# Another order for the eight chunks of the MLP down products: pairs 2 and 3 are multiplied last

## The chip, the cores and the metric

The kernel runs on one core of a Trainium2 chip. The metric is the device time of one execution in microseconds, and the median of several executions stands for a kernel. The core has a matrix engine (TensorE, PE in the profile; its weight loads are PEld), three engines for elementwise work (VectorE or DVE, ScalarE or ACT, GpSimd or POOL) and SyncE (SP), whose queue issues most of the transfers between the chip's memory (HBM) and the core's own memory (SBUF). PE writes its sums to a small memory of eight banks (PSUM). Each engine works through its own list of instructions in order. An instruction that waits holds up all that stand behind it on its engine.

## The reference, cut to what matters

One decoder layer over 2048 tokens of width 1024: a token mixer (an mLSTM beside an attention with latent keys), then an MLP, both between RMS norms. The change concerns the last line but one, the product with `w_down` (4096 x 1024).

```python
x = x + rmsnorm(mix, norm_post_mix[l])
m = rmsnorm(x, norm_pre_mlp[l])
y = jnp.square(jax.nn.relu(m @ w_up[l])) @ w_down[l]
x = x + rmsnorm(y, norm_post_mlp[l])
```

## The kernel before

All products are made in pieces of fp32r numbers: a matrix is split into a high part and a low part, and a product is three matmuls (high by high, high by low, low by high). The products of the MLP follow a scheme of Strassen and Winograd: the 2 x 2 blocks of a product take seven block products and some additions, before and behind.

The hidden width of 4096 is cut into 16 **pairs** `p` of two 128-wide blocks. The up phase (`up`) computes for each pair and each half `g` of the tokens the seven left factors that the down product needs, and stores them in HBM as `hd[p, g]`. For most pairs they are stored **whole**, as fp32 numbers. For the pairs in `TWOS = (2, 6, 10)` they are stored **in two parts**, already split into high and low, which is twice the bytes.

The down phase takes the pairs in eight **chunks** `c` of two (`e` = 0 and 1). A chunk has eight **units** `u`, and a unit makes two tiles of 128 tokens (rows `r` = 0 and 1, each as two halves of 512 columns, named y0_0 to y15_1 by tile and half). Three pieces of code matter:

- `hidden(c, u, e)` brings the seven factors of one pair to SBUF. A pair stored whole is one load (`hr`, 448 KB), then two casts on ACT for the high part (`hh0`, `hh1`, products 0 to 3 and 4 to 6) and two subtractions on DVE for the low part (`hl0`, `hl1`; L2613). A pair stored in two parts is four loads straight into the same tiles (L2597: `hh0` and `hl0` of 256 KB, `hh1` and `hl1` of 192 KB) and no work on ACT or DVE. Each of these tiles has two buffers, so a load or a cast waits until PE has used the tile of two units before.
- `down(c, u, ws)` issues the seven products 0 to 6 of a unit, six matmuls each (three for each pair), into three banks: X (products 0, 4, 5 and 6), Y (1 and 3) and Z (2). A sum in a bank is read by `into`, an addition on DVE into the result (`y<-d_..`, L2681), or by `aside`, a copy on ACT and an addition on POOL (L2696). Product 4 goes on in bank X behind product 0, product 5 behind 4, and 6 behind 5, so each of them waits until the one before has been read. In the last chunk's last unit all of this goes to DVE.
- `finish` runs in the last chunk only, once for each of the 16 tiles: two squares with sums on ACT, a power on POOL (L2745), then for 13 of the tiles two multiplications on DVE (`both`, L2754) and two accumulating stores on the POOL queue (L2757). The last three tiles (14, 11 and 15) get instead a gain (L2735, on POOL for tile 14), two additions on DVE (L2748) and plain stores on the SP queue (L2751).

The right factors, the weights of the next chunk, are made by `first_factors` on ACT (L2371) and DVE (L2341, L2374) while a chunk runs.

What comes when is set by a planner (`Plan`): each operation has an estimated duration, what it follows, the buffers it takes and a key, and the planner goes through a simulated time and picks for each engine the ready operation with the lowest key. Its choice is the order on each engine. The order of PE's products in the down phase is written out by hand (`line`): unit by unit 0, 1, then product 5 of the unit before, 2, 3, product 6 of the unit before, 4. Only the last unit differs: 0, 1, product 5 of the unit before, 4, 2, product 6 of the unit before, 5, 3, 6.

Of the kernel before, what the change touches and what calls it, by code (L numbers as in the profile page):

```python
# [47 lines left out]
EXL = 1.0  # L48
DWIDE = 128
PM_ = 2  # L50
FRESH = (5, 6, 7, 8, 12)
SPREAD = 60.0
LATE = 2000
# [206 lines left out]
def trunk(ctx: ExitStack, tc: tile.TileContext, x, xT, pos, wu, wout, wup, wdn, cols, rows, consts, edge, out, dbg=None):  # L260
# [11 lines left out]
    def sb(stack, name, bufs, side="left"):  # L272
        return stack.enter_context(tc.tile_pool(name=name, bufs=bufs, side=side, reuse_waits="tile"))

    def pp(stack, name, bufs, side="left"):
        return stack.enter_context(tc.tile_pool(name=name, bufs=bufs, side=side, space=PSUM, reuse_waits="tile"))
# [251 lines left out]
    def wsplit(b, u):  # L528
        if u == 0:
            return wboth(b)  # L530
        fresh = b == NB - 1 and u in FRESH
        if b > STB[u] and not fresh:
# [993 lines left out]
    def switch2():  # L1526

        s_x.close()
        pm.append(pp(pc, "pm", PM_))
        V[0] = sb(pc, "a3", 1).tile([P, NT, 4, 129], F32R, tag="V0", name="V0")  # L1530
# [20 lines left out]
    for name, bufs, when in (  # L1551
        ("q", 1, o_s1), ("m", PM_, o_s2), ("S", SB_, o_s3), ("o0", PO_, o_s3), ("o1", 1, o_s3), ("t", TB_, o_s3), ("th", 1, o_s3), ("tl", 1, o_s3), ("ph", HB_, o_s3), ("p", 1, o_s3), ("pl", LB_, o_s3), ("ot", 1, o_s3), ("ou", 1, o_s3),
        ("mp", 4, o_s1), ("mx", 2, o_s1), ("mr", 2, o_s1), ("rsm", 2, o_s3),
# [111 lines left out]
    def maxima(h, qb, keys):  # L1665
# [4 lines left out]
        def ring(i):  # L1670
            return "q" if (h, qb) in EARLY or i % (1 + PM_) == PM_ else "m"

# [901 lines left out]
    def hidden(c, u, e):  # L2574

        g, i = divmod(u, 4)
        p = 2 * c + e
        t = {}
        key = DN + 9.7 * (8 * c + u) + 2 * e
        first = c == 0 and u < 2  # L2580
# [64 lines left out]
    def down(c, u, ws):  # L2645
        g, i = divmod(u, 4)
        s = 8 * c + u
        key = DN + 9.7 * (8 * c + u)
        hs = [hidden(c, u, e) for e in range(2)]
        t = {}  # L2650
        nm = f"d{c}_{u}"
# [129 lines left out]
    for c in range(NCH):  # L2781
        ws = []
        for e in range(2):
            p = 2 * c + e
            ring = [f"w{WORDER[(14 * c + 7 * e + j) % (WB + W2B)]}" for j in range(7)]
            ws.append(first_factors(f"d{p}", DN + 77.6 * c + 3 * e, lambda e_, p=p: wdn[(2 * p + e_) * P : (2 * p + e_ + 1) * P, :], "down", ring, [o_w[KD - 1, 1]]))
        XP["rings"] = [f"w{WORDER[(14 * NCH + k) % (WB + W2B)]}" for k in range(WB + W2B - 14)]
        for u in range(8):
            down(c, u, ws)
# [77 lines left out]
def build(arrays, dbg=None):  # L2867
    import concourse.bacc as bacc

    nc = bacc.Bacc("TRN2", target_bir_lowering=False, num_devices=1)  # L2870
    args = [
        nc.dram_tensor(f"in_{n}_dram", v.shape, mybir.dt.from_np(v.dtype), kind="ExternalInput").ap() for n, v in arrays.items()
    ]
    out = nc.dram_tensor("out_0_dram", (SEQ, DM), F32, kind="ExternalOutput").ap()
    with tile.TileContext(nc) as tc:
        trunk(tc, *args, out, dbg=dbg)
    return nc
# [9 lines left out]
```

## Time and profile before

| | us |
|---|---|
| median of 3 runs (2381.45 to 2382.77) | 2382.29 |
| the profiled execution, its own time | 2380.29 |
| its span, first to last instruction | 2378.5 |
| granted TensorE clock, mean | 0.997 |
| ACT busy in the span | 1353.1 (57%) |
| POOL busy in the span | 813.1 (34%) |
| first matmul of the down phase, start | 1745.85 |

The profile is of one execution. A page gives the busy time of each engine over the whole span; the trace behind it can be asked for a stretch of time, for one engine's instructions in order, or for who waited for whom. Of rows that stand for one instruction the first number is its start, counted from the start of the span, and the second its duration in us. Names have lost their running numbers there: `d_6X` is bank X of unit 6 of whichever chunk runs, `d_7X` of unit 7.

### The profile page before, as it was taken

Reading aid. Unit: us, or ns where it says so; the run is one execution under the profiler, and the core shown is the slowest. Engines: PE = TensorE matmul, PEld = TensorE weight load, DVE = VectorE, ACT = ScalarE, POOL = GpSimd, SP = SyncE. Lnnn points to the kernel's source line nnn. Section 1 sums busy time; section 2 is a strip of 40 time slices with the busy share of each in tenths; the row PEclk is TensorE's granted clock in tenths of the full one; section 3 lists DMA queues with packets and bytes.
Section 4 is the critical chain, followed back from the end, with each engine's and each line's share of the span. In section 5 each row is a group of like instructions: output and inputs, shape, how many; then the busy total and the mean of one; then the engine's idle time right before and its main releaser. Section 6 shows DMA issues by size and latency. Waiting matters only on the chain.

```text
span 2378.5 us, 33991 instructions
## 1 busy us (share of the span) xinstructions
PE 2339.0 (98%) x10989; PEld 1894.3 (80%) x10989; DVE 1717.6 (72%) x3057; ACT 1353.1 (57%) x2581; POOL 813.1 (34%) x697
## 2 busy tenths in 40 slices
PE   9999999999999999999999999999999999999997
PEld 7777778777777777788788888888888888888885
DVE  6767665868888988548667778676675677776778
ACT  5636463447788878344666557656565343443454
POOL 1725343538888888222000000000000223222346
PEclk9999999999999999999999999999999999999999
DMA  7787979783522322667677797665664445345348
GB/s 282 237 315 253 330 261 335 222 205 83 132 65 65 82 49 51 197 218 264 214 233 230 220 289 239 197 178 165 196 202 142 143 142 177 125 148 169 129 138 171
DMA packets 341159, 445.34 MB, mean 187 GB/s; under 512 B 35730, under 2 KB 228174, under 8 KB 340974
## 3 DMA queue, kind: packets, MB, share of 16 engines
q1 hardware_dynamic: 337236, 436.35, 58.8%
q0 software_dynamic: 3744, 6.82, 2.0%
q8 instruction: 86, 1.41, 0.2%
q14 instruction: 93, 0.76, 0.1%
HBM read 291.79 MB, written 153.07 MB: 187 GB/s over the span
## 4 chain that ended last, share of the span: by engine, by line
PE 55%; DVE 1%; DMA 0%; issue 0%; ACT 0%; POOL 0%; DVEq 0%; SPq 0%; POOLq 0%; ACTq 0%
PE op L268 1%; PE op L270 1%; PE op L269 1%; PE d_4X L2658 1%; PE d_1X L2659 1%; PE d_2X L2658 1%; PE d_4X L2659 1%; PE d_3X L2659 1%; PE d_1X L2658 1%; PE d_3X L2658 1%; PE d_2X L2659 1%; PE d_1X L2660 1%; PE d_2X L2660 1%; PE d_3X L2660 1%; PE d_4X L2660 1%; PE d_6X L2658 1%
## 5 line engine op out<-in xcount | busy, mean ns | idle before, releaser
L2696 POOL TENSOR_TENSOR y<-vd_0X,y 128x512 f32<-128x512 f32 x7 | 10.6, 1518 | 726.7 <-ACT vd_0X L2693 726.7
L1813 POOL TENSOR_TENSOR t<-t,ph 128x512 f32<-128x512 f32 (+3 forms) x184 | 209.6, 1139 | 16.8 <-ACT ph L1776 6.7
L1776 ACT ACTIVATE ph<-S 128x512 fp32r<-128x512 f32 (+1 forms) x288 | 165.2, 573 | 80.5 <-PE S L270 29.4
L2608 ACT CAST hh<-hr 128x512 fp32r<-128x512 f32 (+1 forms) x208 | 116.4, 567 | 156.4 <-PE d_5X L2659 15.1
L1784 DVE TENSOR_TENSOR pl<-S,ph 128x512 fp32r<-128x512 f32 (+1 forms) x229 | 153.0, 671 | 35.0 <-ACT S L1780 28.8
L1695 DVE TENSOR_REDUCE mp<-m 128x1 f32<-128x512 f32 (+3 forms) x208 | 136.0, 665 | 26.9 <-PE m L1688 24.3
L2613 DVE TENSOR_TENSOR hl<-hr,hh 128x512 fp32r<-128x512 f32 (+1 forms) x208 | 133.2, 647 | 30.3 <-ACT hh L2608 23.7
L268 PE MATMUL mm<-xh,wh 128*128 128x512 f32 x352 | 143.4, 407 | 4.8 <-DVE gate L1257 3.0
L270 PE MATMUL mm<-xh,wl 128*128 128x512 f32 x352 | 138.0, 392 | 0.7 <-DVE wl L552 0.5
L269 PE MATMUL mm<-xl,wh 128*128 128x512 f32 x352 | 138.0, 392 | 0.0
L1780 ACT ACTIVATE S<-S 128x512 f32<-128x512 f32 (+1 forms) x229 | 133.9, 585 | 0.0
L268 PE MATMUL S<-QK 97*128 97x512 f32 (+2 forms) x320 | 119.2, 373 | 0.3 <-DVE pl L1784 0.2
L1798 PE MATMUL o<-ph,V 128*128 128x512 f32 (+2 forms) x320 | 117.4, 368 | 1.1 <-DVE ot L1872 0.8
L269 PE MATMUL S<-QK 97*128 97x512 f32 (+2 forms) x320 | 117.0, 366 | 0.0
L270 PE MATMUL S<-QK 97*128 97x512 f32 (+2 forms) x320 | 116.5, 364 | 0.0
L1688 PE MATMUL m<-QK 96*128 96x512 f32 (+3 forms) x320 | 112.5, 386 | 2.9 <-DVE mp L1695 1.9
L1801 PE MATMUL o<-pl,V 128*65 128x512 f32 (+2 forms) x320 | 112.5, 361 | 1.1 <-POOL pl L1784 1.1
L268 PE MATMUL op<-wo,hh 128*128 128x512 f32 x256 | 101.0, 394 | 0.1
L270 PE MATMUL op<-wo,hl 128*128 128x512 f32 x256 | 99.8, 390 | 0.0
L269 PE MATMUL op<-wo,hh 128*128 128x512 f32 x256 | 99.8, 390 | 0.0
L2447 ACT ACTIVATE t<-t 128x512 f32<-128x512 f32 x96 | 60.7, 632 | 65.0 <-DVE t L2442 64.5
L268 PEld LDWEIGHTS mm<-xh,wh 128*128 128x128 f32 x352 | 66.1, 188 | 21.3 <-DVE gate L1257 4.7
(6463 smaller groups left out, 7477.3 us busy)
## 6 DMA issues: line engine op xcount, KB each, us to landing
hr<-hd SPq DMA_DIRECT2D x100, 448.0 KB
wr<-in_wu_dram SPq DMA_DIRECT2D x68, 512.0 KB
hd<-t SPq DMA_DIRECT2D x128, 256.0 KB
hd<-ts SPq DMA_DIRECT2D x96, 256.0 KB
wl<-wparts SPq DMA_DIRECT2D x37, 512.0 KB
QK<-qkd SPq DMA_DIRECT2D x32, 512.0 KB
xt<-in_x_dram SPq DMA_DIRECT2D x28, 512.0 KB
xf<-xd SPq DMA_DIRECT2D x40, 256.0 KB
```

The costliest lines, as they stand in the source:

```text
L268: pe.matmul(o, ah, bh, start=start, stop=False)
L269: pe.matmul(o, ah, bl, start=False, stop=False)
L270: pe.matmul(o, al, bh, start=False, stop=stop)
L1695: vec.tensor_reduce(mp["t"][:, j, kb : kb + 1], ps[:, :n], axis=AX.X, op=ALU.max)
L1776: act.activation(t["h"][:, :w], t["S"][:, :w], AF.Exp)
L1780: act.activation(t["p"][:, :w], t["S"][:, :w], AF.Exp)
L1784: (pool if by_pool else vec).tensor_tensor(t["l"][:, :w], t["p"][:, :w], f32(t["h"][:, :w]), ALU.subtract)
L1798: pe.matmul(o0, v[:, 0:128], t["h"][:, c : c + m], start=start, stop=stop)
L1813: pool.tensor_tensor(to, to, f32(t["h"][:, c : c + m]), ALU.add)
L2608: act.copy(t["h", m][:, :w], t["r", m][:, :w])
L2613: vec.tensor_tensor(t["l", m][:, :w], t["r", m][:, :w], f32(t["h", m][:, :w]), ALU.subtract)
L2658: pe.matmul(ps, a, w[:, 0], start=start, stop=False, skip_group_check=True)
```

## The change

The kernel gets a table of eight numbers. Position `c` of the down phase multiplies the pairs 2 * CHUNKS[c] and 2 * CHUNKS[c] + 1, where it multiplied 2c and 2c + 1. The pairs 2 and 3 go from the second place to the eighth, and the six chunks between move up by one. The sums are the same, in another order.

```diff
+CHUNKS = (0, 2, 3, 4, 5, 6, 7, 1)
 ...
     def hidden(c, u, e):
         g, i = divmod(u, 4)
-        p = 2 * c + e
+        p = 2 * CHUNKS[c] + e
 ...
     for c in range(NCH):
         ws = []
         for e in range(2):
-            p = 2 * c + e
+            p = 2 * CHUNKS[c] + e
```

The pairs stored in two parts are 2, 6 and 10, each the first of its chunk. The chunks that hold one were at the places 1, 3 and 5 (counted from 0) and are now at 2, 4 and 7. The order of PE's matmuls is the same row by row, with other factors. The other engines have the same instructions, at other places. Three places are shown; a row gives the line, the operation, and the result and operands with the program's names.

DVE in the last unit of the down phase, before. `y11_0<-d7_7X` is the reading of product 0 of unit 7, `y14_1<-d7_6X` that of product 5 of unit 6.

```order
L2681 TENSOR_TENSOR y10_1_18980<-d7_6X_23611,y10_1_18980 128x512
L2681 TENSOR_TENSOR y10_1_18980<-d7_6Y_23625,y10_1_18980 128x512
L2754 SCALAR_TENSOR_TENSOR y8_0_18760<-y8_0_18760,fsm8_23559,gpm_18466 128x512
L2754 SCALAR_TENSOR_TENSOR y8_1_18824<-y8_1_18824,fsm8_23559,gpm_18466 128x512
L2681 TENSOR_TENSOR y14_1_18920<-d7_6X_23611,y14_1_18920 128x512
L2754 SCALAR_TENSOR_TENSOR y12_0_18885<-y12_0_18885,fsm12_23608,gpm_18466 128x512
L2754 SCALAR_TENSOR_TENSOR y12_1_18768<-y12_1_18768,fsm12_23608,gpm_18466 128x512
L2681 TENSOR_TENSOR y11_0_18994<-d7_7X_23701,y11_0_18994 128x512
```

The same place after the change, where every line number is one higher:

```order
L2755 SCALAR_TENSOR_TENSOR y8_1_18824<-y8_1_18824,fsm8_23512,gpm_18466 128x512
L2682 TENSOR_TENSOR y13_0_18961<-d7_5X_23536,y13_0_18961 128x512
L2614 TENSOR_TENSOR hl1_7_7_1_23722<-hr_7_7_1_23549,hh1_7_7_1_23712 128x384
L2682 TENSOR_TENSOR y10_1_18976<-d7_6X_23630,y10_1_18976 128x512
L2682 TENSOR_TENSOR y10_1_18976<-d7_6Y_23643,y10_1_18976 128x512
L2755 SCALAR_TENSOR_TENSOR y12_0_18885<-y12_0_18885,fsm12_23588,gpm_18466 128x512
L2755 SCALAR_TENSOR_TENSOR y12_1_18768<-y12_1_18768,fsm12_23588,gpm_18466 128x512
L2682 TENSOR_TENSOR y11_0_18990<-d7_7X_23724,y11_0_18990 128x512
L2682 TENSOR_TENSOR y14_1_18920<-d7_6X_23630,y14_1_18920 128x512
```

The reading of product 0 of unit 7 now stands ahead of that of product 5 of unit 6, and the two multiplications for tile 8 stand further ahead. The last addition of all (`y15_0<-d7_7X`) had one multiplication of `both` behind it and now has two, both for tile 10.

DVE at the end of the second chunk, before (this chunk holds a pair in two parts; the rows begin behind the reading of unit 6's bank Y):

```order
L2374 TENSOR_TENSOR d46_19644<-d4s4_19281,d46_19644 128x512
L2341 TENSOR_TENSOR d5s2_19660<-d5r1_19357,d5s1_19393 128x512
L2374 TENSOR_TENSOR d50_19657<-d5r0_19356,d50_19657 128x512
L2613 TENSOR_TENSOR hl0_2_0_1_19683<-hr_2_0_1_19639,hh0_2_0_1_19676 128x512
L2681 TENSOR_TENSOR y14_1_18920<-d1_6X_19564,y14_1_18920 128x512
```

The same place after (this chunk holds two pairs stored whole):

```order
L2375 TENSOR_TENSOR d66_19660<-d6s4_19312,d66_19660 128x512
L2342 TENSOR_TENSOR d7s2_19679<-d7r1_19407,d7s1_19445 128x512
L2682 TENSOR_TENSOR y14_1_18920<-d1_6X_19568,y14_1_18920 128x512
L2614 TENSOR_TENSOR hl0_2_0_1_19699<-hr_2_0_1_19646,hh0_2_0_1_19687 128x512
L2682 TENSOR_TENSOR y11_0_18990<-d1_7Z_19689,y11_0_18990 128x512
```

The reading of bank X has two instructions ahead of it here instead of four. The four stand ahead of it at the end of every chunk with a pair in two parts that another chunk follows: three times before, twice after.

SP at the end of the last chunk, before, ahead of the six plain stores:

```order
L2601 DMA hr_7_5_1_23438<-hd15_1_217 128x896
L2601 DMA hr_7_6_0_23521<-hd14_1_215 128x896
L2601 DMA hr_7_6_1_23537<-hd15_1_217 128x896
L2601 DMA hr_7_7_0_23615<-hd14_1_215 128x896
L2601 DMA hr_7_7_1_23630<-hd15_1_217 128x896
```

And after:

```order
L2602 DMA hr_7_7_1_23549<-hd3_1_193 128x896
L2598 DMA hh0_7_7_0_23599<-hd2_1_191 128x512
L2598 DMA hl0_7_7_0_23605<-hd2_1_191 128x512
L2598 DMA hh1_7_6_0_23611<-hd2_1_191 128x384
L2598 DMA hl1_7_6_0_23621<-hd2_1_191 128x384
L2598 DMA hh1_7_7_0_23705<-hd2_1_191 128x384
L2598 DMA hl1_7_7_0_23710<-hd2_1_191 128x384
```

Each unit's load of its first pair has become four loads, and the last two (for products 4 to 6 of unit 7) stand at the very end of the loads.

## The prediction
> **What bounds the kernel now.** I read the page's busy times first, then the table of busy times by stretch for the down phase, then the waits of PE in it, and last the instructions of PE and DVE in the last unit.
>
> ```profile
> span 2378.5 us, 33991 instructions
> PE 2339.0 (98%) x10989; PEld 1894.3 (80%) x10989; DVE 1717.6 (72%) x3057; ACT 1353.1 (57%) x2581; POOL 813.1 (34%) x697
> ...
> 2132.00:2209.00 77.00, 76.95 (x340) 63.46 (x339) 55.04 (x81) 26.97 (x48) 22.85 (x16) 1.00 0.49 157
> 2209.00:2285.00 76.00, 76.00 (x337) 63.01 (x336) 57.13 (x94) 33.40 (x62) 22.41 (x16) 1.00 0.41 138
> 2285.00:2361.00 76.00, 72.98 (x321) 59.91 (x321) 63.62 (x96) 49.01 (x125) 47.92 (x49) 1.00 0.71 152
> 2361.00:2378.00 17.00, 4.72 (x21) 3.57 (x19) 13.08 (x23) 3.55 (x10) 8.86 (x10) 0.76 0.98 206
> ```
>
> PE is busy for 98% of the span. In the table the columns are the stretch, its length, then PE, PEld, DVE, ACT and POOL, the clock, the DMA share and GB/s. A middle chunk, with or without a pair in two parts (first and second row), leaves PE without a gap that such a table shows. The last chunk does: PE 72.98 of 76 us, DVE at its highest, 63.62. The last 17 us are DVE's. So DVE work is worth something only where PE waits for it:
>
> ```profile
> PE d_7X L2658 <- DVE y L2681: 3.0, 1, 3.0
> ```
>
> This is the only wait of PE that the view names between 1750 us and the end. Its place, in PE's rows:
>
> ```profile
> 2353.90 0.39 PE L2660 MATMUL d_6X<-d,hl 128*128 128x512 f32 x1
> 2357.31 0.47 PE L2658 MATMUL d_7X<-d,hh 128*128 128x512 f32 x1 [3.02 <-DVE y L2681]
> 2357.62 0.39 PE L2659 MATMUL d_7X<-d,hh 128*128 128x512 f32 x1
> ...
> 2365.33 0.39 PE L2660 MATMUL d_7X<-d,hl 128*128 128x512 f32 x1
> ```
>
> Product 4 of unit 7 waits for the reading of its product 0. Why that was late, DVE's rows say:
>
> ```profile
> 2349.99 1.41 DVE L2754 SCALAR_TENSOR_TENSOR y<-y,fsm,gpm 128x512 f32<-128x512 f32 x2
> 2351.31 0.69 DVE L2681 TENSOR_TENSOR y<-d_6Z,y 128x512 f32<-128x512 f32 x1
> 2351.91 0.68 DVE L2681 TENSOR_TENSOR y<-d_6X,y 128x512 f32<-128x512 f32 x1
> 2352.63 0.69 DVE L2681 TENSOR_TENSOR y<-d_6Y,y 128x512 f32<-128x512 f32 x1
> 2353.24 1.40 DVE L2754 SCALAR_TENSOR_TENSOR y<-y,fsm,gpm 128x512 f32<-128x512 f32 x2
> 2354.56 0.68 DVE L2681 TENSOR_TENSOR y<-d_6X,y 128x512 f32<-128x512 f32 x1
> 2355.16 1.40 DVE L2754 SCALAR_TENSOR_TENSOR y<-y,fsm,gpm 128x512 f32<-128x512 f32 x2
> 2356.48 0.68 DVE L2681 TENSOR_TENSOR y<-d_7X,y 128x512 f32<-128x512 f32 x1
> ```
>
> The reading at 2356.48 stands behind the reading at 2354.56 (product 5 of unit 6), which PE finished only with the row at 2353.90 (its end 2354.29), and behind two multiplications. No gap lies between these rows: an addition occupies 0.60 us from start to start, a multiplication 0.66.
>
> **The change, part by part.** The sum is made against the profiled execution (own time 2380.29, span 2378.5).
>
> *The stall goes.* Without it product 4 starts one matmul (0.23 us, the spacing of PE's rows) behind 2353.90, at 2354.13. It started at 2357.31, and the next matmul came 0.08 us later than the spacing: **3.26 us**. In the new order its reading stands ahead of that of product 5. I walk DVE's new list with PE's old times, less 0.3 us (next term):
>
> ```profile
> 2347.24 0.39 PE L2658 MATMUL d_5X<-d,hh 128*128 128x512 f32 x1
> ```
>
> Product 6 of unit 5 starts there and ends six matmuls later, 2348.77 (2347.24 + 5 x 0.227 + 0.39), now 2348.5. Its reading and the last subtraction take DVE to about 2349.7. Product 4 of unit 6 ends 1.36 us (six matmuls) behind product 6 of unit 5, now 2349.9. Then come two additions and two multiplications, to 2352.4, and the reading of product 0 until 2353.1. PE's slot is 2353.8. The margin is 0.7 us. What makes it possible is the work that left the chunk:
>
> ```profile
> L2613 DVE TENSOR_TENSOR hl<-hr,hh 128x512 fp32r<-128x512 f32 x104 | 77.1, 743 | 14.7 <-ACT hh L2608 8.2 <-PE d_4X L2659 3.1 <-PE d_3X L2659 3.1
> L2613 DVE TENSOR_TENSOR hl<-hr,hh 128x384 fp32r<-128x384 f32 x104 | 57.3, 551 | 15.6 <-ACT hh L2608 15.5
> ```
>
> Each unit loses one of each, 8 x (0.743 + 0.551) = 10.4 us of the 63.62. The second chunk gains them. The cover there is PE itself: a chunk of two whole pairs had 57.13 us of DVE in 76 and no PE gap. If that cover failed, each late reading would cost what the next term shows.
>
> *One small gap fewer.* At the end of a chunk with a pair in two parts PE loses a little:
>
> ```profile
> 1898.46 0.39 PE L2660 MATMUL d_7Y<-d,hl 128*128 128x512 f32 x1
> 1898.89 0.50 PE L2658 MATMUL d_6X<-d,hh 128*128 128x512 f32 x1
> 1899.22 0.39 PE L2659 MATMUL d_6X<-d,hh 128*128 128x512 f32 x1
> ...
> 2204.24 0.50 PE L2658 MATMUL d_6X<-d,hh 128*128 128x512 f32 x1
> 2204.57 0.39 PE L2659 MATMUL d_6X<-d,hh 128*128 128x512 f32 x1
> ```
>
> From 1898.46 to 1899.22 pass 0.76 us instead of 2 x 0.227, **0.31 us** lost. It stands three times in the trace, the last time at 2204.24 (again 0.50 us long, with 0.33 to the next), each behind the four-instruction pattern of the order, which now comes twice: 0.31 us saved. PE then ends 3.57 us earlier: at 2365.33 + 0.39 - 3.57 = 2362.15.
>
> *The tail gets longer.* Behind PE's end DVE works without a pause:
>
> ```profile
> 2363.04 0.69 DVE L2681 TENSOR_TENSOR y<-d_7X,y 128x512 f32<-128x512 f32 x1
> ...
> 2364.39 0.69 DVE L2681 TENSOR_TENSOR y<-d_7Y,y 128x512 f32<-128x512 f32 x1 [0.49 <-PE d_7Y L2660]
> ...
> 2366.32 0.69 DVE L2681 TENSOR_TENSOR y<-d_7X,y 128x512 f32<-128x512 f32 x1
> ...
> 2373.29 1.41 DVE L2748 SCALAR_TENSOR_TENSOR y<-y,fsm,fx 128x512 f32<-128x512 f32 x2
> ```
>
> From the last addition to DVE's end, 2374.70, are 8.38 us, and 3.8 more to the span's end for the last store. The new list has one more multiplication there, **+0.66 us**. The last addition began 0.60 us behind PE's end. After the change it depends on a collision. POOL's gain for tile 14 follows the power for that tile, which follows the reading of product 5 of unit 7 on DVE (2363.04, now 2359.5); with 0.6 us for the reading, some 0.9 for the sum and the power, and 1.28 as in the row below, it runs from about 2361.0 to 2362.3. DVE's multiplication for half 1 of tile 13 stands behind the reading at 2364.39, now 2360.8, and would begin at 2361.4. Such a pair stands in the trace:
>
> ```profile
> 2335.32 1.28 POOL L2696 TENSOR_TENSOR y<-vd_5Y,y 128x512 f32<-128x512 f32 x1
> ...
> 2335.88 1.28 DVE L2754 SCALAR_TENSOR_TENSOR y<-y,fsm,gpm 128x512 f32<-128x512 f32 x1
> ```
>
> DVE's took 1.28 us instead of 0.7 and ended 0.56 behind POOL's. Then the multiplication ends at 2362.9, and the last addition starts 0.75 us behind PE's end instead of 0.60: **+0.15 us**. Without the collision it would be about 0.05, so -0.55.
>
> [...]
>
> *The sum:* -3.26 - 0.31 + 0.66 + 0.15 = **-2.76 us**. The four loads instead of one, 448 KB more in each unit, cost nothing if they land in time; the bounds are below. The profiled execution would take 2377.5. The median of the runs lies 2.0 us above the profiled one; on it the forecast is 2382.29 - 2.76 = **2379.5 us**.
>
> **The rivals.**
>
> *No collision.* Then the sum is -3.26 - 0.31 + 0.66 - 0.55 = -3.46, so 2378.8 us. For it: my walk is good to some tenths and the collision needs DVE to come second. Against: POOL has 1.3 us to be hit in.
>
> *The stall stays in part.* The new last unit waits for two loads that were casts before. Product 4 of unit 7 comes three products earlier than in any other unit, and `hl1` is its last load:
>
> ```profile
> 2194.50 0.39 PE L2658 MATMUL d_5X<-d,hh 128*128 128x512 f32 x1
> ...
> 2195.56 0.38 SPq L2597 DMA_DIRECT2D hl<-hd  x1
> ...
> 2331.24 9.67 SPq L2601 DMA_DIRECT2D hr<-hd  x4
> ...
> 2347.02 0.62 ACT L2608 CAST hh<-hr 128x512 fp32r<-128x512 f32 x1 [0.93 <-DMA hr<-hd]
> ```
>
> In the chunk with pair 10, SP issued it 1.06 us behind the start of product 6 of unit 5. Here that is 2347.24 - 0.31 + 1.06 = 2348.0, and PE needs it at 2353.8: 5.8 us. The trace shows no landing of such a load. The nearest is the last of the four `hr`, 448 KB, issued by 2340.6 (2331.24 + 9.67 less 0.32 for itself), for which ACT waited until 2347.02: 6.4 us. So the cost is between 0 and 0.6 us by that; I take 0, since `hl1` has 192 KB. If DVE's margin of 0.7 us also fails, or the moved splits open gaps of 0.31 us at chunk ends, the gain falls to between 0.5 and 2 us: 2380.3 to 2381.8.
>
> [...]
>
> *Slower: the accumulating stores end last.* POOL's order now puts both stores of tile 10 behind the power of tile 15.
>
> ```profile
> 2368.24 0.99 POOL L2757 DMA_DIRECT2D out_dram<-y  x1
> 2368.85 2.23 POOL L2745 TENSOR_TENSOR fsm<-fsm,mhalf 128x1 f32<-128x1 f32 x1
> ...
> out_dram<-y POOLq DMA_DIRECT2D x26, 256.0 KB, 5.2
> ```
>
> The power of tile 15 follows the last addition by about 2 us: 2364.9. With 2.23 us for it, twice 0.99 for the stores and 5.2 to land it ends at 2374.3, ahead of the plain stores at 2375.7. From 1.4 us more on it sets the end, and from 4.2 us more on the kernel is slower than before. If DVE's unbroken run kept POOL out until DVE ends (2371.9), the stores would land at 2371.9 + 2.23 + 1.98 + 5.2 = 2381.3, which is 2.8 us slower than before, 2385.1 us. Against: the two rows above ran inside such a run of DVE.
>
> [...] The 0.99 us of the row, between DVE rows without a gap, speaks for a short delay at most.
>
> **How the numbers follow.** Forecast (2379.0 to 2380.3): 0.42. No collision, or a still shorter tail (2377.5 to 2379.0): 0.25. Stall in part (2380.3 to 2382.3): 0.20. Over 0.2% faster, which needs 4.8 us and so a tail 1.3 us shorter than in the case without the collision, which no term gives: 0.07. Accumulating stores last, 2382.3 and more: 0.06, of which I leave 0.03 for more than 0.2% slower. About 0.2%, 4.8 us, is what a measurement of this kernel can tell from no change. So faster 0.07, the same 0.90, slower 0.03. The range 2377.5 to 2382.3 leaves 0.13 out; the medians scatter by some 0.7 us (2381.45 to 2382.77), so I make it no narrower.
>
> **What would show it.** In the new profile: no wait of PE for DVE in the last unit, or one under 0.6 us; a gap of 0.31 us at two chunk ends instead of three; the last matmul about 3.6 us earlier, the span's end 13.6 us behind it instead of 12.8; DVE's multiplication of tile 13 at 1.3 us beside POOL's gain. The prediction is wrong if PE waits for `hh1` or `hl1` in unit 7, if new PE gaps stand in the second chunk, or if the last transfer to land is one of POOL's.

## The result and the profile after

| | before | after |
|---|---|---|
| median of 22 runs each, us | 2381.96 | 2377.91 |
| ratio, with its 95% interval | 1 | 0.9985 (0.9979 to 0.9991) |
| the profiled execution, its own time | 2380.29 | 2377.90 |
| span | 2378.5 | 2375.4 |
| first matmul of the down phase, start | 1745.85 | 1745.17 |
| from there to PE's end | 619.87 | 616.25 |
| from PE's end to the span's end | 12.78 | 13.98 |

The kernel is faster by 3.6 us by the ratio (2.1 to 5.0, the interval's ends by 2382 us); the two medians differ by 4.05. The forecast was 2.76 us less, at 2379.5 us; the median came 1.6 us below that, inside the stated range and 0.4 us above its lower end. 0.15% is under the 0.2% that one comparison was said to tell, but 22 runs of each separate the two.

First the table of busy times of the changed kernel for the last chunk, the end, and the second chunk (stretch, length, PE, PEld, DVE, ACT, POOL, clock, DMA share, GB/s):

```profile
2285.00:2361.00 76.00, 76.00 (x337) 62.94 (x336) 55.48 (x85) 43.08 (x113) 48.89 (x53) 1.00 0.89 199
2361.00:2375.40 14.40, 0.42 (x2) 0.00 (x0) 10.26 (x16) 1.94 (x6) 5.09 (x6) 0.69 0.83 191
1828.00:1904.00 76.00, 75.88 (x335) 62.52 (x334) 59.82 (x91) 33.50 (x62) 21.26 (x16) 1.00 0.42 137
```

PE has no gap in the last chunk any more: 76.00 of 76, where it had 72.98. DVE has 55.48 us there instead of 63.62, and the DMA engines 0.89 instead of 0.71. The view of PE's waits names none from 1750 us to the end. PE's rows at the place of the old wait, the start of product 4 of unit 7 among them, and PE's last row:

```profile
2352.87 0.39 PE L2661 MATMUL d_6X<-d,hl 128*128 128x512 f32 x1
2353.10 0.39 PE L2659 MATMUL d_7X<-d,hh 128*128 128x512 f32 x1
2353.32 0.39 PE L2660 MATMUL d_7X<-d,hh 128*128 128x512 f32 x1
2353.55 0.39 PE L2661 MATMUL d_7X<-d,hl 128*128 128x512 f32 x1
...
2361.03 0.39 PE L2661 MATMUL d_7X<-d,hl 128*128 128x512 f32 x1
```

And DVE's rows of the last unit, with the tail behind "...":

```profile
2350.55 1.40 DVE L2755 SCALAR_TENSOR_TENSOR y<-y,fsm,gpm 128x512 f32<-128x512 f32 x2
2351.87 0.69 DVE L2682 TENSOR_TENSOR y<-d_7X,y 128x512 f32<-128x512 f32 x1
2353.37 0.69 DVE L2682 TENSOR_TENSOR y<-d_6X,y 128x512 f32<-128x512 f32 x1 [0.81 <-PE d_6X L2661]
...
2360.10 0.69 DVE L2682 TENSOR_TENSOR y<-d_7Y,y 128x512 f32<-128x512 f32 x1 [0.44 <-PE d_7Y L2661]
2360.70 1.71 DVE L2755 SCALAR_TENSOR_TENSOR y<-y,fsm,gpm 128x512 f32<-128x512 f32 x1
2362.34 0.68 DVE L2682 TENSOR_TENSOR y<-d_7X,y 128x512 f32<-128x512 f32 x1
...
2369.97 1.41 DVE L2749 SCALAR_TENSOR_TENSOR y<-y,fsm,fx 128x512 f32<-128x512 f32 x2
```

The reading of product 0 of unit 7 (2351.87) ends 0.54 us ahead of the time at which PE is free for product 4 (2353.10), and DVE then waits for PE (0.81 us), where it was PE that waited. At the end the multiplication of 2360.70 takes 1.71 us, beside POOL's gain for tile 14:

```profile
2360.35 1.51 POOL L2736 TENSOR_TENSOR y<-y,gpm 128x512 f32<-128x512 f32 x1
```

The second chunk lost a little. PE's rows, and then POOL's and DVE's ahead of the reading that PE waited for (1859.00):

```profile
1859.22 0.39 PE L2661 MATMUL d_3Y<-d,hl 128*128 128x512 f32 x1
1859.73 0.50 PE L2659 MATMUL d_2X<-d,hh 128*128 128x512 f32 x1
1860.06 0.39 PE L2660 MATMUL d_2X<-d,hh 128*128 128x512 f32 x1
```

```profile
1856.29 1.63 POOL L2697 TENSOR_TENSOR y<-vd_3Y,y 128x512 f32<-128x512 f32 x1
...
1856.70 1.77 DVE L2375 TENSOR_TENSOR d<-d6s,d 128x512 fp32r<-128x512 f32 x1
1858.40 0.68 DVE L2614 TENSOR_TENSOR hl<-hr,hh 128x512 fp32r<-128x512 f32 x1
1859.00 0.68 DVE L2682 TENSOR_TENSOR y<-d_2X,y 128x512 f32<-128x512 f32 x1
```

From 1859.22 to 1860.06 pass 0.84 us instead of 0.45: 0.38 us lost, at a product whose reading stands behind a split (L2614) that came with the change. The row ahead of the split took 1.77 us instead of 0.68: it ran beside POOL's addition and ended 0.55 us behind it (1858.47 and 1857.92). It is the same kind of collision as at the end.

### The profile page after: what moved, and what is told of

Same layout as the page of the kernel before. It is cut to its first block, busy times and chain, and to the rows that moved or that the text cites. A ratio compares the mean times of both kernels' runs of the same rounds, so it can differ in the third digit from the quotient of the medians.

```text
span 2375.4 us, 34001 instructions
## 1 busy us (share of the span) xinstructions
PE 2338.5 (98%) x10989; PEld 1893.0 (80%) x10989; DVE 1717.7 (72%) x3057; ACT 1354.3 (57%) x2581; POOL 810.1 (34%) x697
## 5 line engine op out<-in xcount | busy, mean ns | idle before, releaser
L2614 DVE TENSOR_TENSOR hl<-hr,hh 128x512 fp32r<-128x512 f32 (+1 forms) x208 | 132.5, 646 | 27.4 <-ACT hh L2609 23.1
L2448 ACT ACTIVATE t<-t 128x512 f32<-128x512 f32 x96 | 60.6, 632 | 64.4 <-DVE t L2443 63.9
L2451 ACT ACTIVATE t<-t 128x512 f32<-128x512 f32 x128 | 80.9, 632 | 3.9
```

The source lines that it names most:

```text
L2614: vec.tensor_tensor(t["l", m][:, :w], t["r", m][:, :w], f32(t["h", m][:, :w]), ALU.subtract)
```

## The experiments

Two theories, and a rival, were set against each other. **Order**: the gain is that one reading got ahead on DVE. **Work**: it is the 10.4 us of splits that left DVE's last chunk. The rival: it matters which pairs come last, not how they are stored. A fourth, **late load**, came up on the way: PE waits for a transfer from HBM. All kernels in one table (us). The ratio is to the kernel before in the same comparison. The last three columns are from one profile each: PE's first matmul of the down phase, from there to PE's end, and the tail, from PE's end to the span's end.

| kernel | median (runs) | ratio (interval) | first | to PE's end | tail |
|---|---|---|---|---|---|
| before | 2381.96 (22) | 1 | 1745.85 | 619.87 | 12.78 |
| after | 2377.91 (22) | 0.9985 (0.9979 to 0.9991) | 1745.17 | 616.25 | 13.98 |
| after, once more | 2378.36 (11) | 0.9982 (0.9973 to 0.9991) | 1746.56 | 616.99 | 13.95 |
| e3: after, other pairs in two parts | 2385.65 (11) | 1.0020 (1.0011 to 1.0029) | 1748.17 | 621.60 | 14.03 |
| e4: before, pair 14 in two parts | 2386.94 (10) | 1.0024 (1.0015 to 1.0033) | 1753.09 | 619.97 | 13.94 |
| c2: before, order fixed | 2385.88 (11) | 1.0017 (1.0008 to 1.0026) | 1749.91 | 621.33 | 13.26 |
| e1: c2 with the reading forward | 2386.49 (11) | 1.0017 (1.0008 to 1.0026) | 1747.83 | 619.70 | 14.07 |
| c1: after, order fixed | 2382.99 (11) | 1.0003 (0.9994 to 1.0012) | 1747.90 | 618.02 | 14.18 |
| e2: c1 with the reading back | 2383.41 (11) | 1.0005 (0.9996 to 1.0014) | 1748.21 | 618.31 | 14.08 |
| e5: after, gain of tile 14 early | 2378.98 (11) | 0.9987 (0.9978 to 0.9996) | 1749.53 | 618.03 | 13.54 |
| e10: after, hl1 early | 2378.57 (11) | 0.9982 (0.9973 to 0.9991) | 1742.99 | 616.26 | 14.25 |
| e9: last chunk wholly in two parts | 2379.71 (11) | 0.9990 (0.9981 to 0.9999) | 1745.99 | 623.04 | 9.47 |
| e11: e9 with three buffers | 2375.46 (8) | 0.9973 (0.9963 to 0.9983) | 1745.67 | 617.59 | 9.94 |
| e12: e11 with the reading first | 2374.70 (7) | 0.9970 (0.9958 to 0.9981) | 1746.25 | 616.86 | 9.89 |

The column "first" is to be read with care: the program ahead of the down phase is the same in after, its repetition, e5 and e10, and it reached the first product between 1742.99 and 1749.53. The scatter arises ahead of the up phase: from the first product of the up phase to the first of the down phase it is 619.23 to 619.47 us in every profile but those of e3 and e4. So a profile speaks for the stretch it shows, and the medians for the whole. An interval of a ratio here is some 0.0009 to either side, 2.1 us, so a median of 11 runs does not tell a difference of 1 us.

### Which pairs come last

e3 is the changed kernel with the splits back in the last chunk; e4 is the kernel before with pair 14 in two parts.

```diff
 e3 (after):   -TWOS = (2, 6, 10)   +TWOS = (4, 8, 12)
 e4 (before):  -TWOS = (2, 6, 10)   +TWOS = (4, 8, 14)
```

> The changed kernel, with the pairs stored in two parts chosen as 4, 8 and 12 instead of 2, 6 and 10, so that the chunks that hold one come at places 1, 3 and 5 of the down phase as in before, and the last chunk holds two pairs stored whole; pairs 2 and 3 are still multiplied last. Theories 'order' and 'work': as before, a wait of PE of 3 us (2.5 to 3.5) in the last unit and the time of before within 1 us (2381 to 2383). Rival 'which pairs come last': as the changed kernel, about 2378, with no wait.

> The kernel before, pairs in their old order 0 to 15, with the pairs stored in two parts chosen as 4, 8 and 14, so that the chunks that hold one come at places 2, 4 and 7 as in the changed kernel. Theories 'order' and 'work': as the changed kernel, no wait of PE in the last unit, 2377 to 2379. Rival 'which pairs come last' (pairs 2 and 3 have lain in memory for long, pairs 14 and 15 have not): as before, 2381 to 2383.

Both medians are above what was expected, so they don't decide between the theories. Other pairs in two parts cost time in the up phase: it takes 622.03 us in e3 and 625.32 in e4, from its first product to the first of the down phase, where before has 619.41. e4's down phase, too, is 3.7 us longer to PE's end than the changed kernel's, by waits in its first chunk and by one in its last. The last chunk tells the theories apart all the same. PE's waits in the down phase, e3:

```profile
PE d_7X L2659 <- DVE y L2682: 3.0, 1, 3.0
PE d_6X L2659 <- DVE y L2682: 0.8, 1, 0.8
PE d_0Y L2659 <- ACT y L2678: 0.2, 1, 0.2
```

and PE's rows of e4 at the same place, product 4 of unit 7:

```profile
2363.55 0.40 PE L2658 MATMUL d_7X<-d,hh 128*128 128x512 f32 x1
2363.78 0.39 PE L2659 MATMUL d_7X<-d,hh 128*128 128x512 f32 x1
2365.06 0.50 PE L2660 MATMUL d_7X<-d,hl 128*128 128x512 f32 x1 [0.89 <-DMA hl<-hd]
```

With pairs 2 and 3 last but stored whole, the wait of 3.0 us is back; with pairs 14 and 15 last and one of them in two parts, PE waits for no reading of DVE there. The rival has fallen. In its place e4 shows another wait: the load of `hl1`, the last one of unit 7, is late.

### The reading moved alone

e1 takes the kernel before, keeps every engine's order, and moves the one reading forward on DVE. e2 takes the changed kernel and moves it back. The order is fixed by a first pass of the planner that only records, and dependencies that chain what it recorded:

```diff
+    log = pl.run(dry=True)
 ...
+    for eng in ("PE", "Activation", "DVE", "Pool", "SP"):
+        seq = [i for e_, i in log if e_ == eng]
+        if eng == "DVE":
+            v = V1[NCH - 1, 7]
+            seq.remove(v)
+            seq.insert(seq.index(BOTH[8, 0]), v)
+        for a_, b_ in zip(seq, seq[1:]):
+            pl.ops[b_][3].append(a_)
```

(e2: `seq.insert(seq.index(V3[NCH - 1, 6]) + 1, v)`.)

> The kernel before with the order of every engine kept, except one instruction: on DVE the reading of product 0 of unit 7 of the last chunk stands directly behind the reading of bank Y of unit 6, ahead of the two multiplications for tile 8. Theory 'order': the changed kernel gains because this reading came free early; then the wait of 3.26 us of PE in the last unit goes (at most 1 us left, at product 5), PE ends 2.3 to 3.3 us earlier and the median is 2 to 3 us below before (about 2379). Theory 'work': the gain is the 10.4 us of splits that left DVE's last chunk; DVE in before is busy from 2347.7 to 2374.7 with gaps of 0.53, 0.67, 0.49 and 0.1 us, so PE ends earlier but the span shrinks by no more than these 1.8 us, and what PE gains over that appears as a longer stretch between PE's end and the span's end (before 12.8 us, then 14 or more).

> The changed kernel with the order of every engine kept, except that on DVE the reading of product 0 of unit 7 stands behind the reading of product 5 of unit 6 again, as in before. Theory 'order': PE waits at product 4 of unit 7 again, by the rows (reading at 2353.37 for 0.69 us, then another 0.6 us, against PE's slot at 2353.1) for 1.3 to 1.7 us, and the time is 1 to 1.7 us above the changed kernel's. Theory 'work': nothing of DVE's work has come back, the wait is taken up by DVE's idle time and the span's end moves by less than 0.5 us.

Both were slower than expected by either theory, so two controls fix the order and move nothing (the same code without the four lines from `if eng` on):

> Control for the run with the reading moved back: the changed kernel, its own order of every engine fixed by the same means, and nothing moved. If the fixing is neutral, the profile has no wait of PE in the down phase and the time is that of the changed kernel (2376 to 2380). If the fixing itself costs (by what the run with the reading moved back showed ahead of the down phase, 3 us), the first product of the down phase starts at about 1748 instead of 1745 us and the median is 2381 to 2382; then 1.5 to 2 us are left for the reading that was moved.

> Control for the run in which the reading was moved forward: the kernel before, its own order fixed by the same means, and nothing moved. The wait of 3 us of PE in the last unit stays. If the fixing is neutral the median is that of before (2381 to 2382); if it costs, 2384 to 2386, and the move itself then changed the time by less than 2 us either way, which is theory 'work'.

Fixing the order costs 5.1 us (c1 against after, 2382.99 - 2377.91; 4.3 by the ratios) and 3.9 us (c2 against before). In these two profiles 1.8 and 1.5 us of it stand in the down phase, by a late load in c1 and by slow matmuls in c2, and nothing in the up phase (619.23 and 619.26 us). Ahead of that the profiles scatter too much to place the rest, so why it costs is not settled. Against its control, e1 gains nothing: the same ratio, 1.0017. The intervals would leave room for some 3 us, but the profiles agree: from the first product of the down phase to the span's end it is 633.77 us in e1, 634.59 in c2 and 632.65 in the kernel before. e1's profile says where the gain went. PE's waits in the down phase, and DVE's rows in the last unit, with one of POOL's:

```profile
PE d_7X L2661 <- DVE y L2684: 2.2, 2, 1.5
```

```profile
2355.53 0.68 DVE L2684 TENSOR_TENSOR y<-d_7X,y 128x512 f32<-128x512 f32 x1
2356.13 1.40 DVE L2759 SCALAR_TENSOR_TENSOR y<-y,fsm,gpm 128x512 f32<-128x512 f32 x2
2357.45 0.68 DVE L2684 TENSOR_TENSOR y<-d_6X,y 128x512 f32<-128x512 f32 x1
...
2360.64 0.68 DVE L2684 TENSOR_TENSOR y<-d_7X,y 128x512 f32<-128x512 f32 x1
...
2361.45 1.95 POOL L2740 TENSOR_TENSOR y<-y,gpm 128x512 f32<-128x512 f32 x1
...
2361.84 2.12 DVE L2759 SCALAR_TENSOR_TENSOR y<-y,fsm,gpm 128x512 f32<-128x512 f32 x1
2363.88 0.68 DVE L2684 TENSOR_TENSOR y<-d_6X,y 128x512 f32<-128x512 f32 x1
...
2365.14 0.68 DVE L2684 TENSOR_TENSOR y<-d_7X,y 128x512 f32<-128x512 f32 x1
```

Product 4 no longer waits, but products 5 and 6 do, 0.67 and 1.49 us, for the next two readings of the same bank (2360.64 and 2365.14). DVE is never idle in between, as theory "work" has it: the wait only moves. The second of the two has a further cause. The multiplication at 2361.84 took 2.12 us instead of 0.74, beside POOL's gain, and ended 0.56 us behind it; in the kernel before, the same gain (2358.55 to 2360.49) met additions from the banks and no multiplication. Without these 1.38 us most of the second wait would be gone. So e1 shows that the exchange gained nothing here; that it can't gain the 1.8 us which DVE was idle in the kernel before is not shown. In the changed kernel the reading moved back does bring a wait of 1.45 us for DVE, as "order" had it, but the time is that of its control within the intervals. The control's own profile has a wait at the same product, for another reason:

```profile
2356.44 0.40 PE L2663 MATMUL d_7X<-d,hh 128*128 128x512 f32 x1
2357.92 0.50 PE L2664 MATMUL d_7X<-d,hl 128*128 128x512 f32 x1 [1.09 <-DMA hl<-hd]
```

Two waits at one product lie over each other, and to PE's end it is 618.31 us in e2 and 618.02 in c1. So this pair can't say what the order is worth in time; it shows only that with the old order the wait for DVE is back.

### The late load

`hl1` again, as in e4. In c1 its load was issued at 2350.11 and let PE go on at 2357.92: 7.8 us. In the changed kernel it was issued at 2347.36 and needed at 2353.55, 6.2 us later, and PE did not wait. So the changed kernel was profiled once more, and with a buffer of its own for this tile:

```diff
+    pl.ring("l0x", 1, o_dr)
 ...
+            if (c, u, e) == (NCH - 1, 7, 0):
+                tags["l", 1] = "l0x"
 ...
```

> The changed kernel once more, unchanged, for a second profile of it. Theory 'late load': the three other kernels with the changed kernel's last unit (order fixed; gain of tile 14 early; old order of pairs with 4, 8 and 14 in two parts) had PE wait 0.9 to 1.1 us for the last load of unit 7 (hl1), so the changed kernel's own profile without a wait was a lucky one, and this one shows 0 to 1.2 us there. If that wait belongs to the edits instead, it is absent again. The start of the down phase (1745.2 in the first profile) shows by how much the program ahead of it varies between executions; the others had 1745 to 1750. Median 2377 to 2380.

> The changed kernel with a buffer of its own for the hl1 tile of the last unit's first pair (192 KB), so that its load does not wait for PE to be done with the tile of unit 5 and is issued long before. All else is in the same order. Theory 'late load': no wait of PE for hl1; what is left is a wait for hh1, issued 0.4 us ahead of hl1 in the changed kernel, of 0 to 0.3 us; PE ends 1.0 us earlier than in profiles that had the wait, and the median is 0.3 to 1 us below the changed kernel's. Theory 'order': no gain, since DVE sets the last unit: its readings then come to stand in PE's way by 0.5 us or more.

Both profiles are without a wait of PE in the last chunk (to PE's end 616.99 and 616.26, against 616.25). So the load was in time in both profiles of the changed kernel, and late in three other kernels with the same last unit (e4, c1, and e5 below, with 1.02 us for `hl1` and 0.20 for `hh1`). How often it is late in the changed kernel is not shown: e10's median is the changed kernel's within 0.7 us, but the 0.3 to 1 us in question are less than the intervals tell. What sets it late was not found. The stores from POOL around it are issued at the same distance from it, and from issue to use the share of the DMA engines is 0.99 to 1.01 in all five profiles. Between 2 and 4 us behind the issue it is 0.77 to 0.84 where the load was late and 0.90 and 0.95 where it was not; five profiles are too few to call that a cause.

### The collision at the end

```diff
-  ... [sq[-1], o_dw], key - GKEY)
+  ... [sq[-1], o_dw], key - (GKEY if end == 2 else 60))
```

> The changed kernel with one piece of work earlier on POOL: its gain for tile 14 stands ahead of the power for tile 14, so that it no longer runs beside DVE's multiplication of tile 13. DVE's list is the same. By the collision theory that multiplication takes 0.74 us instead of 1.71, or meets POOL's gain at an earlier place where DVE has idle time; the last addition starts 0.05 to 0.2 us behind PE's end instead of 0.92, and the time is 0.7 us below the changed kernel's (2377.2). If DVE's 1.71 us had another cause, the last addition stays 0.9 us behind and the time too. What stands ahead of the last unit is the same program, so its times show the scatter between executions.

The multiplication and POOL's gain, from DVE's and POOL's rows of e5:

```profile
2366.85 1.07 DVE L2755 SCALAR_TENSOR_TENSOR y<-y,fsm,gpm 128x512 f32<-128x512 f32 x1
2367.84 0.68 DVE L2682 TENSOR_TENSOR y<-d_7X,y 128x512 f32<-128x512 f32 x1
```

```profile
2365.16 0.86 POOL L2758 DMA_DIRECT2D out_dram<-y  x1 [1.86 <-DVE y L2755]
2365.73 1.62 POOL L2736 TENSOR_TENSOR y<-y,gpm 128x512 f32<-128x512 f32 x1
```

The gain began 1.12 us ahead of the multiplication instead of 0.35, held back by a store that waited for DVE, so the multiplication still met its end: 1.07 us instead of 1.71. The last addition began 0.28 us behind PE's end (2367.56) instead of 0.92, and the tail is 13.54 us instead of 13.98. That is the direction expected, and 0.4 of the 0.7 us in the tail, but the gain did not get out of the multiplication's way. The median (0.9987 against 0.9985) can't show so little, and PE's waits for the late load, 1.2 us, stand against it in this profile. In both kernels DVE's operation ended 0.55 to 0.57 us behind POOL's (2362.41 and 2361.86; 2367.92 and 2367.35), whenever it had begun. So it is POOL's end that these rows follow, and not a fixed stretch. In the kernel before, two multiplications that began 0.25 and 0.32 us ahead of POOL's addition took 0.75 and 0.74 us (2304.32 and 2342.40), but one that began 0.77 us ahead, while POOL issued two stores, took 3.25 (2326.29) and ended 0.56 us behind the addition. POOL's rows took 1.51 and 1.62 us instead of 1.28, which is not accounted for; they overlap the rows ahead of them, so their starts are rough.

### Both pairs of the last chunk in two parts

```diff
 e9:   -TWOS = (2, 6, 10)   +TWOS = (2, 3, 6)
 e11, on top of it:
+            if TWO[p] and m and c == NCH - 1 and u in (2, 5):
+                a = pl.op("SP", 1000, both_parts, [*op_, *o_hd[p, g]], key - 6, take=("hr2",), kb=384)
 ...
 e12, on top of that:
+    for e in range(2):
+        pl.ops[BOTH[10, e]][3].append(V1[NCH - 1, 7])
```

> The changed kernel with the pairs 2, 3 and 6 stored in two parts instead of 2, 6 and 10: both pairs of the last chunk need no split, and only one other chunk holds such a pair. DVE's last chunk loses another 8 x (0.74 + 0.55) = 10.4 us of work. PE has no wait left to lose there, so theory 'order' gives nothing for PE and a shorter end alone: behind the last addition stand 6 additions of the reference's residual (L2749), 2 gains and 3 small operations, 6.0 to 6.4 us instead of 9.04, so the span ends 2 to 2.7 us sooner behind PE's end, unless the stores or the loads of four parts twice (0.9 MB more in each unit's two loads) become late: then PE waits for them in the last chunk. The up phase splits other pairs than before, which cost 2 to 7 us in the two runs that did so; so the whole time is 2376 to 2384, and the reading is taken from PE's end on.

e9's tail is 4.5 us shorter than the changed kernel's, more than expected: 6.42 us from the last addition (2369.07) to DVE's end (2375.49) are as expected, but the addition also follows PE's end by only 0.04 us, and the span's end comes 1.0 us sooner behind DVE's (3.0 instead of 4.0). PE lost more than that, 6.8 us (623.04 against 616.25):

```profile
2358.08 0.50 PE L2661 MATMUL d_7X<-d,hl 128*128 128x512 f32 x1 [0.86 <-DMA hl<-hd]
2359.65 0.78 PE L2659 MATMUL d_7X<-d,hh 128*128 128x512 f32 x1 [1.07 <-DMA hh<-hd]
2360.23 0.63 PE L2660 MATMUL d_7X<-d,hh 128*128 128x512 f32 x1
2360.65 0.63 PE L2661 MATMUL d_7X<-d,hl 128*128 128x512 f32 x1
```

Two loads of unit 7 are late here, a third one in unit 5 (0.87 us), and behind them the matmuls are 0.63 us long and 0.43 apart instead of 0.39 and 0.23.

> The kernel of the run with both pairs of the last chunk in two parts, with the loads for products 4 to 6 of units 2 and 5 of the last chunk put into the two buffers of the whole pairs (hr), which are idle there. So each such tile has three buffers in turn and its load is issued a unit (9.5 us) earlier in units 4, 6 and 7. Theory 'late load': the three waits of PE (0.87, 0.86 and 1.07 us) and the slow matmuls behind the last (1.9 us) go, PE ends 3.5 to 4.5 us earlier in relation to the start of the down phase, the stretch from PE's end to the span's end stays near 9.5 us, and the median is 2375 to 2377. If the DMA engines are full in the last chunk, so that an earlier issue only queues longer, the waits stay at 0.5 us or more each and the time stays near 2379.

The waits for loads are gone, and with them the slow matmuls (the granted clock is 1.00 from 2285 to 2364 us): to PE's end 617.59 us instead of 623.04. One wait for DVE came in their place, of the old kind, behind a multiplication that itself waited for POOL:

```profile
2353.40 0.75 DVE L2766 SCALAR_TENSOR_TENSOR y<-y,fsm,gpm 128x512 f32<-128x512 f32 x1 [0.59 <-POOL fsm L2757]
2354.06 0.68 DVE L2693 TENSOR_TENSOR y<-d_7X,y 128x512 f32<-128x512 f32 x1
```

> The kernel of the run with three buffers, with one exchange on DVE and nothing else moved: the reading of product 0 of unit 7 stands ahead of the multiplication of half 0 of tile 10, which waited 0.59 us for its power there. It is the same kind of edit as the reading moved forward in the kernel before, but here DVE has idle time around it (0.67, 0.12, 0.59 and 0.65 us in the unit). Theory 'order, once DVE has room': the wait of PE for DVE (0.92 us, 1.08 with the longer matmul behind it) goes, no other appears, PE ends 1.0 to 1.1 us earlier from the start of the down phase (616.5 us instead of 617.6), the last addition stays 0.05 us behind PE's end, and the median is 0.8 to 1.1 us below that run (2374.4 to 2374.7). Theory 'work' alone: the wait comes back at product 5 or 6, or at the end, and the time stays at 2375.5.

In e12 the reading stands ahead, and DVE's idle time takes up what is put behind it:

```profile
2352.45 1.42 DVE L2767 SCALAR_TENSOR_TENSOR y<-y,fsm,gpm 128x512 f32<-128x512 f32 x2
2353.78 0.68 DVE L2693 TENSOR_TENSOR y<-d_7X,y 128x512 f32<-128x512 f32 x1
2354.46 0.75 DVE L2767 SCALAR_TENSOR_TENSOR y<-y,fsm,gpm 128x512 f32<-128x512 f32 x1
```

PE waits for nothing in the last chunk. To its end it is 616.86 us, with 0.45 us lost at 1747.95 that e11 did not lose; so by these two profiles the edit gave 1.2 us in the down phase (617.59 - 616.86 + 0.45), about as expected. The median of 2374.70 is 0.76 us below e11's; the intervals of the two overlap. Both are faster than the kernel before beyond doubt (0.9970 and 0.9973). In the comparison that it shares with the changed kernel's repetition, e11 is 2.9 us below it (2375.46 against 2378.36).

## Why the prediction was right, and where it was not

- **The stall goes (3.26 us): right**, in both profiles of the changed kernel and in e10. The walk of DVE's list had the reading done 0.7 us ahead of the time PE needs it; it was 0.54. With the old work and the new order PE still waits 2.2 us (e1, in part by a collision), with the new work and the old order 1.45 us (e2), and not at all with both. Where DVE has idle time, the exchange by itself removes the wait (e12). All this is read from profiles; the medians do not tell these cases apart.
- **One small gap fewer (0.31 us): right for the chunk ends, wrong for the sum.** Two of them are left. But new gaps in the second chunk were named as a sign that the prediction is wrong, and there is one. The step that costed the splits moved into the second chunk at nothing, with PE as their cover, failed by 0.38 us at 1859.73, and another 0.18 us stand in the seventh chunk (2231.93). What it left out is the collision: in both places a DVE operation of 0.68 us took 1.77 or 1.78 beside an addition on POOL, just ahead of the reading. Before had 0.15 us of such gaps, so gaps as a whole came out 0.10 us larger instead of 0.31 smaller.
- **The tail (0.66 + 0.15 us): right in its parts, 0.39 us short in size.** From the last addition to DVE's end it is 9.04 us instead of 8.38, which is the 0.66. The collision came where it was expected, but the multiplication took 1.71 us, not 1.28, and the last addition followed PE's end by 0.92 us instead of the 0.75 forecast. The span's end added 0.2 us that was not in the sum.
- **Account of the profile**: PE's end came 4.30 us earlier (2361.42 against 2365.72): 3.26 from the stall, 0.68 from the program ahead of the down phase and 0.45 from a gap at 1747.55 in before's profile that has to do with neither (the second profile of the changed kernel has one there again), less 0.10 from the gaps. The tail took back 1.20. What belongs to the change is -3.26 + 0.10 + 1.20 = -1.96 us by this one pair of profiles, with the forecast at -2.76; the difference is the two terms above, 0.41 for the gaps and 0.39 for the tail.
- **The medians say more than that, -4.05 and -4.25 us** (2378.36 against 2382.61 in the second comparison; by the ratios' intervals -2.1 to -5.0 and -2.1 to -6.4). With the order fixed in both kernels the same change gave -2.9 us (c1 against c2, in one comparison). Two things that the one profile of before did not show go in that direction. Its tail of 12.78 us is the shortest of the four profiles with such a last chunk (c2 13.26, e3 14.03, e1 14.07), and so is its last part, from DVE's end on: 3.80 us against 4.28, 5.04 and 4.83. And the stall can cost more than itself: in c2 it is followed by slow matmuls that lose another 1.7 us (3.49 us for eight spacings of 0.227; last section). How often the kernel before does so was not measured, so the rest is open.
- **Where luck had a part.** The median of 2377.91 lies in the band 2377.5 to 2379.0, which the prediction gave 0.25 for a missing collision or a shorter tail. The collision was there and the tail was longer than forecast, so the median came there for other reasons: 0.3 us because the kernel before has its median at 2381.96 over 22 runs and not at 2382.29, and the rest by what the last point leaves open.
- **The rivals.** The stall in part, by a late load, is real as a mechanism. Its price was set too low: 7.2 to 7.8 us from issue to use where it was late, against the 6.4 taken as a bound from a larger load, so PE waited 0.9 to 1.2 us instead of 0 to 0.6. In the changed kernel itself it did not come in two profiles; the load had 6.2 us there, where 5.8 were forecast. "No collision" did not happen. The accumulating stores did not end last: the last two were issued by 2367.0 (2365.19 + 1.79), and the chain that ended last runs through DVE's additions.

## What to carry to other kernels

An instruction moved ahead on an engine that has no idle time hands its wait on to the instructions behind it (in e1 from product 4 to products 5 and 6, 0.67 and 1.49 us); look first whether work can leave the stage, and then where idle time lies to take up the exchange. Storing operands ready for use trades an engine's work for transfers: the gain comes in full only when the buffers let the loads start early enough, which e9 (2379.71) and e11 (2375.46) show with the same work. A term of 0.2 to 0.5 us read from one profile can lie within what executions of the same program differ by (616.25 and 616.99 us to PE's end in two of the changed kernel); a second profile of the kernel before, had it been taken, could have told which of its 12.78 us of tail and of its small gaps are its own. And a new order can bring the work of two engines side by side: here DVE operations of some 0.7 us took 1.07 to 2.12 us beside an operation of POOL.

## What the runs showed of the hardware

A stop of PE can cost more than its length: in c2 it is 3.0 us, and 1.7 more in the slow matmuls behind it. Tables of busy times in c2, the stop and what follows, and in the kernel before:

```profile
2358.20:2361.22 3.02, 0.01 (x2) 0.04 (x1) 3.02 (x6) 2.52 (x8) 2.28 (x4) 1.00 1.04 147
2361.22:2364.70 3.48, 3.48 (x8) 2.74 (x9) 1.69 (x3) 0.07 (x1) 3.48 (x5) 0.51 1.11 172
2364.70:2371.20 6.50, 6.50 (x29) 5.07 (x27) 4.97 (x10) 1.92 (x5) 3.81 (x5) 1.00 0.89 142
```

```profile
2357.31:2360.80 3.49, 3.49 (x16) 2.90 (x17) 2.29 (x4) 0.07 (x1) 3.49 (x5) 1.00 1.06 174
```

Behind the same stop of 3.0 us the granted clock is 0.51 for 3.48 us in c2 (8 matmuls), and 1.00 in before (16 in 3.49 us) and in e3 (15 in 3.46 us). In e9 it is 0.52 for 3.55 us behind two waits of 0.86 and 1.07 us with a few matmuls around them. So the slow stretch of some 3.5 us came behind stops of 3.0 us and less; what sets it off, and why it is there in one execution and not in another, these profiles do not show.

The other surprise is the last load: 192 KB took 7.2 to 7.8 us from issue to use in e4, c1 and e5, with the DMA engines' share at 0.98 to 1.01 over the 7.5 us behind the issue. POOL's accumulating stores held 81% of the 16 engines' time in e5 over the 7.8 us. In the changed kernel's first profile they held 79% over the 6.2 us, and the load was in time.
